# A two-layer conditioned trunk on one core: first shift vector summed with moving weight rows, and the convolution's shifted copies made by SBUF transfers

## The chip, the cores and the metric

The kernel runs on one core of a Trainium2 chip. The engines are TensorE (PE, with weight loads listed as PEld), VectorE (DVE), ScalarE (ACT), GpSimd (POOL) and SyncE (SP), which here only issues transfers. The metric is the device time in us of one execution, the median of the runs of a program. The kernel before took 1071.75 us (three runs, 1071.41 to 1072.74).

## The reference

Two layers over x of 256 positions by 1024 channels, float32. Each layer has three sub-layers on a modulated RMS norm: a SwiGLU feed-forward with half weight, a mixer, and a second feed-forward. The mixer of layer 0 is block attention with one block of 256 (its block selection is empty at this length), that of layer 1 is a Conformer convolution.

```python
c_act = jax.nn.silu(c)
mod = (c_act @ ada_w[i] + ada_b[i]).reshape(B, N_SUB, 3, D_MODEL)   # shift, scale, gate
pre(z, j) = rms_norm(z, norm_g[i, j]) * (1.0 + scl[:, j]) + shift[:, j]
x = x + 0.5 * gate[:, 0] * swiglu_ffn(pre(x, 0), ffn_w_in[i, 0], ffn_w_out[i, 0])
x = x + gate[:, 1] * mixer(pre(x, 1))
x = x + 0.5 * gate[:, 2] * swiglu_ffn(pre(x, 2), ffn_w_in[i, 1], ffn_w_out[i, 1])

def conformer_conv(h, ...):
    a, g = jnp.split(h @ w_pw1 + b_pw1, 2, axis=-1)
    u = a * jax.nn.sigmoid(g)
    u = depthwise_causal_conv(u, w_dw, width=31) + b_dw
    u = jax.nn.silu(layer_norm(u, ln_g, ln_b))
    return u @ w_pw2 + b_pw2
```

## The kernel before

All weights pass once through one ordered list, the stream, of tiles of 128 x 1024 float32 (512 KB) called `raw`, with six buffers. Python code sets the order by hand: `weave` mixes weight tiles with tiles of the modulation matrix `ada_w`, and each entry of the stream is issued on SP's queue as soon as the tile six places earlier is used up (`issue`, L188 to L204). `step` uses one entry: for a weight, ScalarE rounds it into a high part `whi` (L243) and VectorE subtracts to get the low part `wlo` (L218), so that `mm3` (L608 to L610) makes a float32 product of three rounded ones; for a modulation tile, VectorE folds its rows, weighted with silu(c), into `acc` (L279, L281). `need(unit)` steps until a unit is split, `block()` takes as many further steps as the current quota (`take(n)`) allows, and `run_sums` lets TensorE add up the 128 partitions of a finished `acc`. Split weights have a ring of six.

The start (`start`, `early_fold`, `early_sum`, `early_transposes`, `early_turn`) makes the first scale and shift vectors in four quarters of 256 columns. For each quarter four tiles arrive: scale rows in two tiles, shift rows in two, and then three weight tiles. VectorE folds both scale tiles and the first shift tile (twelve operations, L477 and L479). For the last shift tile TensorE takes each 128 x 128 piece as weights and one column of silu(c) as the moving side (L499). A matmul with a column of ones adds the partitions of `acc` (L500). In the first quarter `idle` puts matmuls on dummy data between these.

The convolution (`conv`) works on eight blocks of 128 channels. Blocks 0 to 3 are projected with positions on the partitions (`UT`) and turned (`across`), blocks 4 to 7 directly (`U`), into one of two PSUM banks `u`. `glu` applies sigmoid on ScalarE (L1009) and the product on VectorE (L1010) and writes `ub`, 128 channels by 288 positions with 30 zeros ahead. `spread` makes, for each group of 32 channels, four copies shifted by 0 to 3 positions on four partition groups of `R` (16 copies a block, eleven on VectorE, L1024, five on ScalarE, L1022). `wide` makes the filter tile `wd` on GpSimd (L963): taps on a diagonal mask. The depthwise block `C` is then 32 matmuls, each four taps times 32 channels against one channel group of `R` (L1033), and ScalarE adds the bias into `v`. `VT` transposes `v`; statistics, `norm`, `swish` and `put` prepare the input of the output projection `O`. Three buffers `ub`, two each of `R`, `wd` and `v`. The order of the loop over blocks:

```python
glu(b + 2); C(b); spread(b + 2); U(b + 4); wide(b + 2); VT(b - 1)
```

The second shift vector of layer 1's last feed-forward, `ada(4, (1, 2, 0))`, is woven between the convolution's weights.

## Time and profile before

| | |
|---|---|
| median of three runs | 1071.75 us |
| profiled execution, its own time | 1072.88 us |
| its span, first to last instruction | 1071.0 us |
| mean granted TensorE clock | 0.98 |
| busy: PE, PEld, DVE, ACT, POOL | 97%, 80%, 76%, 47%, 5% |
| HBM read | 248.24 MB, 233 GB/s over the span |

The busy shares are means over stages. The granted clock says how fast TensorE was allowed to run, as a share of 2.4 GHz; 0.5 is the lower level of 1.2 GHz. Durations of matmuls overlap, so the time that a group of them takes is read from where the group starts to where the next one starts.

### The profile page before, as it was taken

The numbers are of one execution on the slowest core, as the hardware profiler recorded it, in microseconds if no ns is written. First come the engines' busy times: TensorE is split into PE (matmuls) and PEld (weight loads), VectorE is DVE, ScalarE is ACT, GpSimd is POOL, SyncE is SP. The second block draws the span as 40 slices with busy tenths as digits, with TensorE's granted clock in tenths as the row PEclk, the third lists the DMA queues.
The fourth block names the chain that finished last, engine by engine and source line by source line (L and its number), as shares of the span: only waits on it lengthen the run. The fifth ranks groups of instructions, "written<-read, shape, count | busy, mean of one in ns | idle before, by whom it ended". The sixth has DMA issues, their size and how long they took to land.

```text
span 1071.0 us, 14807 instructions
## 1 busy us (share of the span) xinstructions
PE 1038.3 (97%) x5522; PEld 853.5 (80%) x5522; DVE 815.1 (76%) x1267; ACT 503.8 (47%) x794; POOL 53.2 (5%) x83
## 2 busy tenths in 40 slices
PE   8999999999999999999999999999988799999998
PEld 6888888877777788888878888888867588888886
DVE  5878878878997798778568788776789768665643
ACT  3354444555676544344354444454555446434430
POOL 3000000001210000000020000000211100000000
PEclk8999999999999999999999999999988899999999
DMA  8979998948767399898728889885545227776711
GB/s 297 297 244 340 307 324 296 332 160 260 248 205 221 101 324 313 281 311 293 251 88 311 284 296 317 284 289 159 164 149 195 86 65 238 270 230 199 236 40 39
DMA packets 181692, 250.26 MB, mean 234 GB/s; under 512 B 8389, under 2 KB 132070, under 8 KB 181620
## 3 DMA queue, kind: packets, MB, share of 16 engines
q1 hardware_dynamic: 180784, 248.55, 69.6%
q0 software_dynamic: 688, 0.71, 0.3%
q8 instruction: 43, 0.70, 0.2%
q14 instruction: 29, 0.24, 0.1%
q10 hardware_dynamic: 148, 0.06, 0.0%
HBM read 248.24 MB, written 1.05 MB: 233 GB/s over the span
## 4 chain that ended last, share of the span: by engine, by line
PE 87%; DVE 8%; issue 2%; ACT 1%; DMA 1%; POOL 1%; SPq 0%; DVEq 0%; POOLq 0%; ACTq 0%
PE u L608 15%; PE u L610 15%; PE u L609 14%; PE y L608 11%; PE y L610 11%; PE y L609 11%; DVE R L1024 2%; DVE wlo L218 2%; PE m L686 2%; PE m L322 1%; PE m L1033 1%; DMA raw<-in_ada_w_dram 1%; PE m L499 1%; DVE x L545 1%; PE m L587 1%
## 5 line engine op out<-in xcount | busy, mean ns | idle before, releaser
L218 DVE TENSOR_TENSOR wlo<-raw,whi 128x1024 fp32r<-128x1024 f32 x320 | 382.4, 1224 | 31.2 <-ACT whi L243 31.0
L243 ACT ACTIVATE whi<-raw 128x1024 fp32r<-128x1024 f32 x320 | 328.5, 1054 | 164.2 <-DMA raw<-in_ffn_w_in_dram 97.7
L608 PE MATMUL u<-whi,hh 128*128 128x512 f32 x672 | 266.5, 397 | 0.0
L610 PE MATMUL u<-whi,hl 128*128 128x512 f32 x672 | 262.7, 391 | 0.0
L609 PE MATMUL u<-wlo,hh 128*128 128x512 f32 x672 | 261.8, 390 | 0.0
L281 DVE SCALAR_TENSOR_TENSOR acc<-raw,sc,acc 128x512 f32<-128x512 f32 x224 | 169.5, 757 | 5.6 <-DMA raw<-in_ada_w_dram 0.7
L610 PEld LDWEIGHTS u<-whi,hl 128*128 128x128 f32 x672 | 126.1, 188 | 28.4 <-DVE hl L603 1.2
L608 PEld LDWEIGHTS u<-whi,hh 128*128 128x128 f32 x672 | 126.3, 188 | 25.5 <-ACT hh L602 0.6
L609 PEld LDWEIGHTS u<-wlo,hh 128*128 128x128 f32 x672 | 126.4, 188 | 25.1
L608 PE MATMUL y<-whi,gh 128*128 128x512 f32 x352 | 138.8, 394 | 0.2 <-ACT gh L694 0.2
L610 PE MATMUL y<-whi,gl 128*128 128x512 f32 x352 | 137.3, 390 | 0.0
L609 PE MATMUL y<-wlo,gh 128*128 128x512 f32 x352 | 137.1, 389 | 0.0
L695 DVE TENSOR_TENSOR gl<-m,gh 128x512 fp32r<-128x512 f32 (+1 forms) x48 | 31.1, 647 | 93.0 <-ACT gh L694 92.8
L608 PE MATMUL y<-whi,hh 128*128 128x512 f32 (+1 forms) x256 | 98.2, 384 | 0.0
L609 PE MATMUL y<-wlo,hh 128*128 128x512 f32 (+1 forms) x256 | 94.9, 371 | 0.0
L610 PE MATMUL y<-whi,hl 128*128 128x512 f32 (+1 forms) x256 | 94.7, 370 | 0.0
L694 ACT ACTIVATE gh<-m 128x512 fp32r<-128x512 f32 (+1 forms) x48 | 27.0, 562 | 132.4 <-PE m L686 132.4
L656 ACT ACTIVATE sg<-u 128x256 f32<-128x256 f32 x84 | 32.1, 382 | 113.9 <-PE u L610 113.9
L610 PEld LDWEIGHTS y<-whi,gl 128*128 128x128 f32 x352 | 66.1, 188 | 14.6 <-DVE gl L695 0.4
L608 PEld LDWEIGHTS y<-whi,gh 128*128 128x128 f32 x352 | 66.1, 188 | 13.8 <-ACT gh L694 0.7
L609 PEld LDWEIGHTS y<-wlo,gh 128*128 128x128 f32 x352 | 66.1, 188 | 13.3
L657 DVE TENSOR_TENSOR g<-u,sg 128x256 f32<-128x256 f32 x84 | 35.5, 422 | 35.0 <-ACT sg L656 34.6
(157 smaller groups left out, 984.4 us busy)
## 6 DMA issues: line engine op xcount, KB each, us to landing
raw<-in_ffn_w_in_dram SPq DMA_DIRECT2D x164, 512.0 KB, 5.0
raw<-in_ada_w_dram SPq DMA_DIRECT2D x144, 512.0 KB, 5.0
raw<-in_ffn_w_out_dram SPq DMA_DIRECT2D x88, 512.0 KB, 5.1
raw<-in_attn_w_qkv_dram SPq DMA_DIRECT2D x24, 512.0 KB, 4.8
raw<-in_conv_w_pw_dram SPq DMA_DIRECT2D x24, 512.0 KB, 4.9
raw<-in_ffn_w_in_dram SPq DMA_DIRECT2D x24, 256.0 KB, 5.5
raw<-in_attn_w_o_dram SPq DMA_DIRECT2D x8, 512.0 KB, 4.6
gate<-in_ada_b_dram SPq DMA_DIRECT2D x6, 512.0 KB, 6.7
```

The source lines that it names most:

```text
L218: (eng or nc.vector).tensor_tensor(lo, raw, hi.bitcast(F32), op=ALU.subtract)
L243: self.nc.scalar.activation(hi, self.like(self.raws[i], hi), AF.Copy)
L281: nc.vector.scalar_tensor_tensor(dst, raw[:, i, :], self.sc[:, k : k + 1], dst, op0=ALU.mult, op1=ALU.add)
L608: nc.tensor.matmul(out, lh, rh, start=start, stop=False)
L609: nc.tensor.matmul(out, lh, rl, start=False, stop=False)
L610: nc.tensor.matmul(out, ll, rh, start=False, stop=stop)
L656: nc.scalar.activation(sg, ps[:, 0:256], AF.Silu)
L657: nc.vector.tensor_tensor(gs[c][:, t, :], ps[:, 256:512], sg, op=ALU.mult)
L686: nc.tensor.transpose(ps[:, o : o + P], g[:, t, k * P : k * P + P], self.ident)
L694: nc.scalar.activation(hi, src, AF.Copy)
L695: nc.vector.tensor_tensor(lo, src, hi.bitcast(F32), op=ALU.subtract)
L1024: nc.vector.tensor_copy(dst, src)
```

## The change

In the start, only the two scale tiles are folded on VectorE. Both shift tiles stand as the moving side of TensorE: silu(c) is spread to 32 equal columns (`sc32`), which are the weights, and the 256 columns of a row block move through one of four column groups. The four partial rows (on partitions 0, 32, 64, 96) are copied to SBUF by ScalarE (`br`), and a matmul with the selecting column `pick` adds them and turns them onto partitions. The first quarter gets a second group of four idle matmuls. The two tiles of x are issued one weight tile earlier each.

In the convolution, `spread` issues 16 transfers from SBUF to SBUF, half on SP's queue, half on POOL's; `ub` and `R` get four buffers, `wd` and `v` three. All four gates of the first blocks come before the loop; the loop runs over four blocks and starts with the projection; the depthwise blocks 5, 6 and 7 are split into halves of 128 positions, each with a PSUM bank of its own. `b2` (the output bias) uses a buffer of the gates. The convolution's weights come first in the stream, and the eight tiles of the shift vector `(1, 2, 0)` last. The pad tile and the area for POOL's DMA descriptors get smaller.

```diff
--- before.py
+++ after.py
@@ -173,7 +173,9 @@
-        weave(pw1 + pw2, ada(4, (1, 2, 0)), 3)
+        for u in pw1 + pw2:
+            put(u)
+        stream.extend(ada(4, (1, 2, 0)))
...
         for i in range(RAW):
+            if i == 1:
+                nc.sync.dma_start(self.x[0], a["x"][0, 0:P, :])
-                nc.sync.dma_start(self.x[0], a["x"][0, 0:P, :])
-            if i == 3:
...
+        self.sc32 = self.fp.tile([P, KT, 64], F32, name="sc32")[:, :, 0:32]
+        nc.vector.tensor_copy(self.sc32, self.sc.unsqueeze(2).to_broadcast([P, KT, 32]))
+        self.pick = const.tile([P, 1], F32, name="pick")
+        nc.vector.tensor_reduce(
+            self.pick, self.ident.rearrange("p (k c) -> p k c", c=32)[:, :, 0], axis=AX.X, op=ALU.add
+        )
@@ -465,46 +472,61 @@
         nc = self.nc
-        accs = []
-        for e in range(3):
+        acc = self.fp.tile([P, 512], F32, name="acc", tag="acc", bufs=2)[:, 0:256]
+        shift = []
+        for e in range(4):
             raw = self.raws[self.taken].rearrange("p (k n) -> p k n", k=4)
-            if e != 1:
-                acc = self.fp.tile([P, 512], F32, name="acc", tag="acc", bufs=2)[:, 0:256]
-                accs.append(acc)
+            self.taken += 1
+            self.high = max(self.high, self.taken)
+            if e >= 2:
+                shift.append(raw)
+                continue
             for i in range(4):
-                k = 4 * (e % 2) + i
+                k = 4 * e + i
                 if k == 0:
                     nc.vector.tensor_scalar(acc, raw[:, i, :], self.sc[:, k : k + 1], None, op0=ALU.mult)
                 else:
                     nc.vector.scalar_tensor_tensor(
                         acc, raw[:, i, :], self.sc[:, k : k + 1], acc, op0=ALU.mult, op1=ALU.add
                     )
             self.issue()
+        return acc, shift
...
+        def scale(ps):
+            for i in range(2):
+                nc.tensor.matmul(ps[:, i : i + 1], acc[:, i * P : i * P + P], self.one, start=True, stop=True)
+
+        rows = self.bank("m" if q else "y")
+        if not q:
+            ps = self.bank("m")
+            scale(ps)
+        for e, raw in enumerate(shift):
+            if not q:
                 idle(IDLE_SUMS)
...
+            for k in range(4):
+                nc.tensor.matmul(
+                    rows[32 * k : 32 * k + 32, 0:256], self.sc32[:, 4 * e + k, :], raw[:, k, :],
+                    start=e == 0, stop=e == 1,
+                )
+            self.issue()
+        br = self.two.tile([P, 256], F32, name="br", tag="sq", bufs=1)
+        nc.scalar.activation(br, rows[:, 0:256], AF.Copy)
+        pt = self.early_transposes(q)
+        if q:
+            ps = self.bank("m")
+            scale(ps)
+        for i in range(2):
+            nc.tensor.matmul(ps[:, 2 + i : 3 + i], br[:, i * P : i * P + P], self.pick, start=True, stop=True)
...
-        ub = [cp.tile([P, 288], F32, name=f"ub{i}") for i in range(3)]
+        ub = [cp.tile([P, 288], F32, name=f"ub{i}") for i in range(4)]
-        us, R, wd, cs, yv, st, mv, rs = {}, {}, {}, {}, {}, {}, {}, {}
+        us, R, wd, yv, st, mv, rs = {}, {}, {}, {}, {}, {}, {}
-            wd[b] = cp.tile([P, 8, 4, 32], F32, name="wd", tag="wd", bufs=2)
+            wd[b] = cp.tile([P, 8, 4, 32], F32, name="wd", tag="wd", bufs=3)
@@ -1013,21 +1035,17 @@
         def spread(b):
-            u = ub[b % 3]
-            R[b] = cp.tile([P, 4, 284], F32, name="R", tag="R", bufs=2)
+            u = ub[b % 4]
+            R[b] = cp.tile([P, 4, 284], F32, name="R", tag="R", bufs=4)
             for g in range(4):
                 for j in range(4):
-                    dst, src = R[b][32 * j : 32 * j + 32, g, :], u[32 * g : 32 * g + 32, j : j + 284]
-                    if 4 * g + j in (1, 4, 7, 10, 13):
-                        nc.scalar.activation(dst, src, AF.Copy)
-                    else:
-                        nc.vector.tensor_copy(dst, src)
+                    eng = nc.sync if (g + j) % 2 else nc.gpsimd
+                    eng.dma_start(R[b][32 * j : 32 * j + 32, g, :], u[32 * g : 32 * g + 32, j : j + 284])
         def C(b, t0=0, n=T):
-            if b not in cs:
-                cs[b] = self.bank("m")
-                us["v", b] = cp.tile([P, T], F32, name="v", tag="v", bufs=2)
-            ps = cs[b][:, t0 : t0 + n]
+            if ("v", b) not in us:
+                us["v", b] = cp.tile([P, T], F32, name="v", tag="v", bufs=3)
+            ps = self.bank("m")[:, 0:n]
             for q in range(8):
                 for g in range(4):
                     nc.tensor.matmul(
...
-        b2 = cp.tile([P, D], F32, name="b2")
+        b2 = self.two.tile([P, D], F32, name="b2", tag="gate")
...
-        wide(0), wide(1)
@@ -1115,44 +1132,40 @@
         UT(w[1][:, 256:], 2, 1)
         across(0, 1, e, 0), across(1, 1, e, 256)
         e = evac(w[1])
-        glu(0), spread(0)
+        glu(0), spread(0), wide(0)
         UT(w[3][:, 256:], 3, 1)
         f = evac(w[3])
         across(2, 0, e, 0), across(2, 1, e, 256)
-        glu(1), spread(1)
+        glu(1), spread(1), wide(1)
+        across(3, 0, f, 0), across(3, 1, f, 256)
+        glu(2), spread(2), wide(2)
+        glu(3), spread(3)
         take(PUMP_LOOP)
-        for b in range(6):
-            if b >= 4:
-                self.block()
-            if b:
-                glu(b + 2)
+        for b in range(4):
+            U(b + 4)
+            glu(b + 4)
             C(b)
-            if not b:
-                across(3, 0, f, 0), across(3, 1, f, 256)
-                glu(b + 2)
-            spread(b + 2)
-            if b + 4 < 8:
-                U(b + 4)
-            wide(b + 2)
+            spread(b + 4), wide(b + 3)
             if b:
                 VT(b - 1)
-            if b == 1:
-                nc.vector.tensor_tensor(b2, b2, gate, op=ALU.mult)
-            elif b in (2, 3):
-                x = self.x[b - 2]
-                nc.vector.tensor_tensor(x, x, b2, op=ALU.add)
+                if b == 1:
+                    nc.vector.tensor_tensor(b2, b2, gate, op=ALU.mult)
+                else:
+                    x = self.x[b - 2]
+                    nc.vector.tensor_tensor(x, x, b2, op=ALU.add)
         nc.scalar.activation(warm, self.mhalf, AF.Silu)
-        self.need(self.pw2[2])
+        self.block()
+        C(4), wide(7), VT(3)
+        self.need(self.pw2[3])
+        take(5)
+        C(5, 0, P), VT(4), self.block(), C(6, 0, P), VT(5, (0,)), C(7, 0, P), VT(6, (0,))
+        C(5, P, P), VT(7, (0,)), moments(0), norm(0, 0), norm(0, 1)
         take(0)
-        C(6, 0, P), VT(5), C(7, 0, P), C(6, P, P), VT(6, (0,)), VT(7, (0,))
-        moments(0), norm(0, 0), norm(0, 1)
-        C(7, P, P), VT(6, (1,)), swish(0, 0), VT(7, (1,)), moments(1), put(0, 0)
+        C(6, P, P), VT(5, (1,)), C(7, P, P), VT(6, (1,)), swish(0, 0), VT(7, (1,)), moments(1), put(0, 0)
+        self.run_sums(True)
         swish(0, 1), norm(1, 0), put(0, 1), norm(1, 1)
         O(0, 0), swish(1, 0), O(0, 1), put(1, 0), swish(1, 1), put(1, 1), take()
-        O(0, 2)
-        self.need(self.pw2[3])
-        self.run_sums(True)
-        O(0, 3)
+        O(0, 2), O(0, 3)
         self.residual(0, y[0], gate, 1.0)
         O(1, 0), O(1, 1)
         after()
...
-    nc = _bacc.Bacc("TRN2", target_bir_lowering=False, num_devices=1)
+    nc = _bacc.Bacc("TRN2", target_bir_lowering=False, num_devices=1, dynamic_dma_scratch_size=8192)
```

Three places show what moves. On POOL, between the set-up of the convolution's buffers and its statistics, before (`ub` is the gated input, `b` the output bias, `wd` the filter):

```order
L956 MEMSET ub_6567 128x30
L957 MEMSET ub_6567 128x2
L1100 DMA b_6575<-in_conv_b_pw_dram 128x1024
L963 TENSOR_TENSOR wd<-w_4927,mask 128x1024 x8
L1059 TENSOR_TENSOR lr_7683<-lr_7683,mhalf 128x1
```

The same place now:

```order
L1118 DMA b_6578<-in_conv_b_pw_dram 128x1024
L1043 DMA R<-ub_6565 32x284 x8
L985 TENSOR_TENSOR wd<-w_4927,mask 128x1024
L1043 DMA R<-ub_6566 32x284 x8
L985 TENSOR_TENSOR wd<-w_4927,mask 128x1024
L1043 DMA R<-ub_6567 32x284 x8
L985 TENSOR_TENSOR wd<-w_4927,mask 128x1024
L1043 DMA R<-ub_6568 32x284 x8
L1043 DMA R<-ub_6565 32x284 x8
L985 TENSOR_TENSOR wd<-w_4927,mask 128x1024
L1043 DMA R<-ub_6566 32x284 x8
L985 TENSOR_TENSOR wd<-w_4927,mask 128x1024
```

Each filter now stands behind the eight transfers of a block; the filters of blocks 3 to 6 stand behind the transfers of the block after them.

On VectorE, from the gate of block 0 to that of block 3, before (`wlo` is the low part of a split weight, `acc` a fold):

```order
L1010 SCALAR_TENSOR_TENSOR ub_6565<-u,cols,sg 128x256
L1024 COPY R<-ub_6565 32x284 x11
L218 TENSOR_TENSOR wlo<-raw,whi 128x8x128 x2
L1010 SCALAR_TENSOR_TENSOR ub_6566<-u,cols,sg 128x256
L1024 COPY R<-ub_6566 32x284 x11
L1010 SCALAR_TENSOR_TENSOR ub_6567<-u,cols,sg 128x256
L1024 COPY R<-ub_6567 32x284 x11
L281 SCALAR_TENSOR_TENSOR acc<-raw,sc,acc 128x512 x2
L218 TENSOR_TENSOR wlo<-raw,whi 128x8x128 x2
L279 TENSOR_SCALAR acc<-raw,sc 128x512
L281 SCALAR_TENSOR_TENSOR acc<-raw,sc,acc 128x512
L218 TENSOR_TENSOR wlo<-raw,whi 128x8x128
```

The same place now:

```order
L1032 SCALAR_TENSOR_TENSOR ub_6565<-u,cols,sg 128x256
L220 TENSOR_TENSOR wlo<-raw,whi 128x8x128 x2
L1032 SCALAR_TENSOR_TENSOR ub_6566<-u,cols,sg 128x256
L1032 SCALAR_TENSOR_TENSOR ub_6567<-u,cols,sg 128x256
L1032 SCALAR_TENSOR_TENSOR ub_6568<-u,cols,sg 128x256
L220 TENSOR_TENSOR wlo<-raw,whi 128x8x128
L220 TENSOR_TENSOR wlo<-raw,whi 128x1024 x4
L1032 SCALAR_TENSOR_TENSOR ub_6565<-u,cols,sg 128x256
```

The four gates follow each other with two splits between them, and no copy is left.

On TensorE, the sums of the second quarter of the first modulation, before (`z` is the normed x, `y` a hidden block's PSUM bank):

```order
L500 MATMUL m<-one,acc 128x1 x2
L499 MATMUL m<-sc,raw 128x1 x4
L500 MATMUL m<-one,acc 128x1
L499 MATMUL m<-sc,raw 128x1 x4
L500 MATMUL m<-one,acc 128x1
L516 MATMUL m<-ident,z 128x128 x4
L608 MATMUL y<-whi,hh 128x512
```

The same place now:

```order
L511 MATMUL m<-raw,sc_158 32x256 x8
L538 MATMUL m<-ident,z 128x128 x4
L501 MATMUL m<-one,acc 128x1 x2
L523 MATMUL m<-pick,br 128x1 x2
L630 MATMUL y<-whi,hh 128x512
```

Eight matmuls with 256 moving columns replace eight with one column and two sums; the selecting matmuls stand behind the transposes and the scale's sums.

## Rows read from the trace of the kernel before

**Rows 1.** the page's first part: busy us of each engine, with its share of the span, and its number of instructions.

```profile
PE 1038.3 (97%) x5522; PEld 853.5 (80%) x5522; DVE 815.1 (76%) x1267; ACT 503.8 (47%) x794; POOL 53.2 (5%) x83
```

**Rows 2.** whom TensorE waited for, over the whole span: engine, line and output tile of the waiting instruction, then engine, tile and line of the one it waited for; us in total, times, longest.

```profile
PE u L608 <- DVE ub L1010: 9.2, 2, 5.0
PE m L1033 <- DVE R L1024: 4.3, 5, 2.6
```

**Rows 3.** windows of the convolution stage: from and to in us of the span, length, busy us (and instructions) of TensorE's matmuls, its weight loads, VectorE, ScalarE and GpSimd, then the granted TensorE clock as a share of full speed, the mean busy share of the DMA engines, and GB/s. 792.05 to 798.22 and 806.91 to 815.75 each hold one projection block and two transposes, 815.75 to 819.34 one depthwise block, and 851.06 to 855.18 what lies between the last depthwise matmul and the first output matmul.

```profile
792.05:798.22 6.17, 6.17 (x54) 6.00 (x51) 5.87 (x12) 5.94 (x10) 1.97 (x1) 1.00 0.41 158
...
806.91:815.75 8.84, 8.84 (x51) 8.67 (x51) 8.59 (x17) 6.43 (x10) 0.00 (x0) 0.65 0.46 147
...
815.75:819.34 3.59, 3.59 (x66) 1.98 (x65) 2.29 (x3) 0.00 (x0) 0.00 (x0) 1.00 0.88 266
...
837.23:851.06 13.83, 12.49 (x261) 9.52 (x261) 8.42 (x25) 5.34 (x12) 0.56 (x1) 0.76 0.04 17
...
851.06:855.18 4.12, 2.59 (x22) 2.00 (x19) 3.75 (x9) 2.84 (x9) 0.55 (x1) 1.00 0.02 4
...
769.72:855.18 85.46, 70.15 (x881) 55.35 (x879) 74.53 (x136) 43.84 (x82) 12.85 (x8) 0.88 0.43 143
```

**Rows 4.** TensorE in order of time, from 771 to 781: start, length, engine, line, operation, output and input tile, shapes, how many; in brackets the idle time before it and what ended it.

```profile
771.68 3.61 PE L1033 MATMUL m<-R,wd 128*32 128x256 f32 x58 [0.37 <-DVE R L1024]
...
775.22 0.66 PE L1001 MATMUL u<-ident,z 128*128 128x128 f32 x4
...
780.04 0.58 PE L608 MATMUL u<-hh,whi 128*128 128x256 f32 x1 [4.16 <-DVE ub L1010]
```

**Rows 5.** VectorE in order of time in the same stretch (columns as in the group before).

```profile
767.44 0.48 DVE L1010 SCALAR_TENSOR_TENSOR ub<-u,cols,sg 128x256 f32<-128x256 f32 x1 [2.68 <-ACT sg L1009]
...
773.84 0.48 DVE L1010 SCALAR_TENSOR_TENSOR ub<-u,cols,sg 128x256 f32<-128x256 f32 x1
...
774.42 5.05 DVE L1024 COPY R<-ub 32x284 f32<-32x284 f32 x11
```

**Rows 6.** groups of instructions by line between 740 and 900 us: line, engine, operation, tiles, shapes, count, then busy us and mean ns of one, then the idle time before them and what ended it.

```profile
L1024 DVE COPY R<-ub 32x284 f32<-32x284 f32 x88 | 32.6, 370 | 5.4 <-PE m L1033 3.5
...
L1022 ACT ACTIVATE R<-ub 32x284 f32<-32x284 f32 x40 | 17.5, 438 | 18.2 <-DVE ub L1010 17.6
...
L963 POOL TENSOR_TENSOR wd<-w,mask 128x1024 f32<-128x1024 f32 x8 | 15.6, 1955 | 67.7 <-PE m L1033 67.7
...
L993 ACT ACTIVATE z<-y 128x512 f32<-128x512 f32 x4 | 2.4, 592 | 4.5 <-PE y L610 4.5
...
L1009 ACT ACTIVATE sg<-u,cols 128x256 f32<-128x256 f32 x8 | 3.7, 462 | 0.0
...
L1010 DVE SCALAR_TENSOR_TENSOR ub<-u,cols,sg 128x256 f32<-128x256 f32 x8 | 3.8, 480 | 2.7 <-ACT sg L1009 2.7
```

**Rows 7.** GpSimd (POOL) in order of time: the last of nine small transfers at the start, the first four of the loads of the convolution taps, and one filter `wd`.

```profile
10.28 0.49 POOL L385 DMA_DIRECT2D rows<-in_attn_g_k_dram  x1 [1.72 <-DMA ab<-in_ada_b_dram]
...
556.87 2.27 POOL L931 DMA_DIRECT2D tq<-in_conv_w_dw_dram  x4 [0.29 <-POOL tq L927]
...
775.44 1.99 POOL L963 TENSOR_TENSOR wd<-w,mask 128x1024 f32<-128x1024 f32 x1 [18.58 <-PE m L1033]
```

**Rows 8.** DMA issues by line: tiles, issuing queue, count, KB each, median us from issue to landing. The first row is of the window 755 to 860, the second of the whole span.

```profile
raw<-in_conv_w_pw_dram SPq DMA_DIRECT2D x13, 512.0 KB, 4.6
...
tq<-in_conv_w_dw_dram POOLq DMA_DIRECT2D x7, 16.0 KB, 3.4
```

**Rows 9.** the instructions that touch the raw weight tiles in the window 755 to 860: count, then shortest, median and longest in ns, first and last start, shapes.

```profile
L218 DVE TENSOR_TENSOR wlo<-raw,whi x20: 1212/1220/2865, 761.0 to 833.1; 128x1024 fp32r<-128x1024 f32 x20
...
L281 DVE SCALAR_TENSOR_TENSOR acc<-raw,sc,acc x14: 744/752/2397, 758.7 to 813.5; 128x512 f32<-128x512 f32 x14
...
L203 SPq DMA_DIRECT2D raw<-in_conv_w_pw_dram x13: 327/340/368, 759.5 to 811.7; - x13
```

**Rows 10.** the same view for VectorE's copies into the tile `R`.

```profile
L1024 DVE COPY R<-ub x88: 295/300/1926, 768.0 to 844.8; 32x284 f32<-32x284 f32 x88
```

**Rows 11.** groups by line in the window 20 to 60 us (columns as in group 6).

```profile
L479 DVE SCALAR_TENSOR_TENSOR acc<-raw,sc,acc 128x256 f32<-128x256 f32 x30 | 14.5, 485 | 1.1
...
L243 ACT ACTIVATE whi<-raw 128x1024 fp32r<-128x1024 f32 x10 | 10.5, 1052 | 18.4 <-DMA raw<-in_ffn_w_in_dram 18.4
...
L528 ACT ACTIVATE hf<-m,mod,mod 128x256 f32<-128x256 f32 x6 | 3.1, 562 | 4.8 <-PE m L516 4.8
```

**Rows 12.** TensorE in order of time at the sums of the second quarter of the first modulation: the matmuls on the last shift tile for 128 columns, and the sum of VectorE's part.

```profile
28.01 1.03 PE L499 MATMUL m<-sc,raw 128*128 128x1 f32 x8
...
28.90 0.36 PE L500 MATMUL m<-one,acc 128*128 128x1 f32 x2
```

**Rows 13.** windows of the start (columns as in group 3). 30.63 to 35.05, 43.48 to 46.33 and 55.22 to 59.65 hold the twelve matmuls of the third hidden block, one window for each quarter, right behind the sums of the next.

```profile
30.63:35.05 4.42, 4.42 (x15) 3.51 (x14) 3.48 (x6) 2.60 (x4) 0.00 (x0) 0.61 0.90 285
...
35.05:40.49 5.44, 5.44 (x25) 4.50 (x24) 5.08 (x13) 0.65 (x1) 0.00 (x0) 1.00 1.00 336
...
43.48:46.33 2.85, 2.85 (x16) 2.34 (x15) 2.04 (x4) 2.51 (x4) 0.00 (x0) 1.00 0.83 257
...
55.22:59.65 4.43, 4.43 (x16) 3.50 (x14) 2.03 (x4) 2.60 (x4) 0.00 (x0) 0.61 0.90 308
```
## What was predicted

> **What bounds the kernel now.** The page's busy shares come first: TensorE is busy for 97% of the span [rows 1], so an edit pays only where TensorE stands still, runs at its low clock, or loses an instruction of its own. The list of who TensorE waited for comes next [rows 2]: two waits for the gated convolution input `ub` make 9.2 us and five for its shifted copies `R` make 4.3 us, all in one stage. So the third view is a table of windows over that stage [rows 3]. From 769.72 to 855.18 it takes 85.46 us, TensorE is busy for 70.15 of them, and the granted clock is 0.88. The longest wait for `ub` is 5.0 us [rows 2], and the projection behind it, 806.91 to 815.75, takes 8.84 us at clock 0.65, where the one in 792.05 to 798.22 takes 6.17 us at 1.00 [rows 3]. A pause is so paid twice: itself, and some 2.5 us at the lower of the two clock levels (1.2 GHz) behind it. Last come the two engines' order of time around the other pause, of 4.16 us [rows 4], and what VectorE does in front of it [rows 5]: `ub` of block 1 ends at 774.3, eleven copies run until 779.47, and only then comes `ub` of block 2, which frees the PSUM bank that the projection of block 4 needs. The page's line groups give the size: 88 copies of 370 ns on VectorE (32.6 us), 40 of 438 ns on ScalarE (17.5 us) [rows 6].
>
> **The convolution, step by step.** The floor is TensorE's own work at full clock. Four projections with a pair of transposes each: 4 x 6.17 = 24.7 us. Eight depthwise blocks: 8 x 3.59 = 28.7 us. Four more transpose pairs of some 0.3 us (6.17 less the 5.9 of a bare projection, an estimate): 1.2. Two groups of transposes into the banks: some 1.0, at 0.66 for four [rows 4]. The tail from the last depthwise matmul to the first output matmul: 4.12 us. One column sum that ran inside a projection before and now stands in the tail: 1.0. Durations without a group are in [rows 3]. Sum 60.7 us, so at most 85.5 - 60.7 = 24.8 us can go.
>
> What is late next? All 128 copies leave both engines and become 128 transfers, 64 on SP's queue and 64 on POOL's, four buffers deep.
>
> POOL first, since it also makes the filters `wd` between them. A POOL transfer costs 0.49 to 0.57 us of issue: four took 2.27 us in one row, a single one 0.49 [rows 7]. A filter takes 1.96 us [rows 6]. A block is 8 x 0.55 + 1.96 = 6.4 us, eight blocks 51 us. Starting when `ub` of block 0 is written (767.9) [rows 5], POOL ends at 819. TensorE consumes a block in 6.17 + 3.59 = 9.8 us, so POOL is ahead in the loop and is met again only at its end, where three depthwise blocks follow without a projection: I allow 1 us there. Each transfer waits for the one eight places earlier to land; landing takes 3.4 us for small ones from POOL [rows 8], less than the 6.4 us of a turn.
>
> SP next: eight transfers a block at about the 0.34 us of a weight issue [rows 9] are 2.7 us, with at most five weight issues behind them (1.7 us), 4.4 of the 9.8 us available. The transfers of block b+4 wait on SP for the depthwise block b, and what is queued behind them is the weights of the next block, six raw tiles ahead of need; nobody waits for those at once. A transfer issued behind weights lands like them, 4.6 us after issue [rows 8]; it is needed three blocks, some 29 us, later. That cover is absent for block 0 alone: its last POOL issue is at 772.3, landing 775.7, filter ready 774.3, while the projection of block 4, in front of its depthwise block, ends near 778. [...]
>
> Then the banks. Projections have two PSUM banks; the gate of block 2 waits for transposes that wait for block 1's. ScalarE's copy (0.6), sigmoid (0.46) and VectorE's product (0.48) [rows 6] make about 1.2 us of pause ahead of the first projection, instead of 4.16.
>
> VectorE keeps 5 steps per block. A split costs 1.22 us, a fold of a late vector's tile 2 x 0.75 [rows 9]: at most 5 x 1.5 = 7.5, with the product 0.48 and up to 2 us held up by a filter some 10 us in the last blocks, against 9.8. The product has a bank in hand, so I take zero; the bound is 2 us. The late vector's steps all stand before the last projection ends, so its sums are ready in the tail.
>
> Each depthwise block now starts behind 16 transfer semaphores, four on each of four matmuls. No row shows such a start; bounds are 0 and the 0.37 us that TensorE lost where it waited for the copies within a block [rows 4], eight times that being 3.0 us. I take 1.5, halfway, since no row is nearer. Losses: 1.0 + 1.2 + 1.5 = 3.7. Gain 24.8 - 3.7 = 21.1 us.
>
> A row speaks on the POOL half in another way. A copy on VectorE takes 0.295 us at least and 1.926 at most [rows 10], and the long ones begin where a filter begins on POOL (775.44) [rows 7]: the two engines held each other up. The Trainium skill, page "SBUF — State Buffer", section "SBUF: two separate sides", says that a VectorE copy in a fast mode and a GpSimd operation exclude each other for the whole instruction, and gives about 3.1 us for a POOL-issued DMA beside such a copy, where one alone takes 0.62. By that, an estimate from the page, 64 issues would cost 198 us. The trace agrees on the filter, and on the tap loads it shows 2.27 us for four issues beside VectorE's splits, with no such stretch [rows 7]; and the change removes the copies. So the sum goes by 0.55.
>
> **The start.** Per quarter of the first modulation, VectorE loses four folds of 0.485 us [rows 11], 1.9 us. TensorE loses eight one-column matmuls and two sums (the trace shows each as two passes), two runs of 1.03 + 0.36 [rows 12]; it gains eight matmuls with 256 columns in groups of 32 (a quarter of the 3.59 us of a depthwise block's 32: 0.9 us) and two sums (0.4). Per quarter 2.8 - 1.3 = 1.5 us less. Against it stands ScalarE's copy `br`, queued ahead of two weight splits of 1.05 us; by the sigmoid of the same size it takes 0.46, so the modulation (two of 0.56 us) [rows 11] starts some 2.5 us after the sums instead of at once. TensorE, with one 2.85 us block as cover [rows 13], stalls about 0.5 us. Two of three quarters also show the low clock behind the one-column matmuls: 4.42 and 4.43 us at 0.61, against 2.85 at 1.00 [rows 13]. I count on getting back half of one, 0.8 us. Weight arrival limits it: the DMA engines are 0.83 to 1.00 busy in these windows [rows 13]. The first quarter is a draw: `x` comes one tile sooner, the second scale tile later, and four more idle matmuls stand on TensorE. Sum: 3 x 1.0 + 0.8 = 3.8 at best in TensorE's terms; with arrival I take 2. Bounds: +2 (first quarter delayed, no clock gained) and -5 (three quarters at 1.5, no drop). The smaller pad and descriptor area and the bias's new place cost nothing: they free space, and the bias is still fetched ahead of the first projection and used in the loop.
>
> Total: 21 + 2 = 23 us. The profiled execution took 1072.88 us for a span of 1071.0; 1072.88 - 23 = 1049.9. The median of the runs is 1.1 us lower, so 1049.
>
> **Rivals.** (1) The transfers become the wait in some blocks. For: weights and copies share the DMA engines, 0.43 busy in the stage before [rows 3], with 4.7 MB more (128 x 32 x 284 x 4 bytes) in less time. Against: four buffers. Two late blocks with 3 us of pause and 2.5 us of low clock each, and 2 us at the start: gain 21 - 11 = 10, time 1062.
>
> (2) POOL sets the pace and the kernel is slower. Behind the last filter stand half blocks of 1.8 us (4 x 1.8), transposes and the tail, 12 us; equal time is reached if the last filter is ready at 843, so (843 - 768 - 8 x 1.96) / 64 = 0.93 us per issue decides. For: the one issue that waited for the transfer eight places earlier stood 1.72 us [rows 7], and this wait now comes 56 times. Against: it stood behind a saturated queue, and 1.72 per turn of eight gives 8.1 us a block, still under 9.8. At 1.2 us an issue: 8 x (9.6 + 1.96) = 92, end at 872, 17 us later: 1089. The skill's rule is the extreme of this case.
>
> (3) The stage shrinks but the time doesn't, since the weights set the pace of what follows. For: DMA was idle from 837 on and TensorE ran on prefetched weights [rows 3]. Against: full buffers then, which are full again. Time 1071.
>
> **Chances.** The forecast 0.66 (its own range 1042 to 1055: 24.8 + 5 off the median at best, 21 - 6 with no gain at the start at worst), rival 1 0.20, rival 2 0.10, rival 3 0.04. The range of 1042 to 1064 takes in rival 1 and leaves out rivals 2 and 3 and a little of the edges. A change under 0.2%, some 2 us, can't be told from none. Faster 0.86, same 0.04, slower 0.10.
>
> **What would show it.** In the profile after: no copies `R` on VectorE or ScalarE; the two waits for `ub` near 1 us; granted clock 0.97 or more and four projections near 6 us; POOL's transfers near 0.55 us with filters between; from the first projection to the first output matmul some 62 us. At the start: eight matmuls of about 0.9 us per quarter, and windows behind them at clock 1.00. A depthwise block that waits for a DMA by microseconds speaks for rival 1, POOL issues over 0.93 us for rival 2, output matmuls that wait for weights for rival 3.

## The result and the profile after

| | median, us | range, us |
|---|---|---|
| kernel before (same chip) | 1071.58 | 1071.10 to 1072.74 |
| changed kernel | 1064.20 | 1063.25 to 1065.08 |

The ratio is 0.9929, with a 95% interval of 0.9912 to 0.9947. The kernel is 7.4 us faster, where 23 were forecast. The profiled execution took 1063.98 us, for a span of 1062.2. Of the runs of the experiments below one, of `half_count`, took 2627.02 us in a slow state and is left out of that kernel's ratio.

The page's busy shares, against [rows 1]:

```profile
span 1062.2 us, 15077 instructions
...
PE 1029.1 (97%) x5590; PEld 839.5 (79%) x5590; DVE 786.7 (74%) x1165; ACT 487.3 (46%) x759; POOL 87.6 (8%) x149
```

Who TensorE waited for, against [rows 2] (us in total, times, longest):

```profile
PE y L1065 <- ACT v L1055: 12.1, 2, 9.1
PE m L708 <- DVE g L679: 4.1, 3, 1.4
...
PE u L630 <- ACT hh L553: 1.2, 3, 0.4
PE u L1023 <- DVE ub L1032: 1.1, 1, 1.1
```

The two waits that the prediction attacked are gone but for the one of 1.1 us that it left. A new one heads the list: a transpose of the depthwise result `v`, twice, 12.1 us. Windows of the convolution stage, cut as in the last row of [rows 3] and up to the first output matmul, and of the end of that stage (columns as there):

```profile
764.96:845.16 80.20, 65.28 (x946) 52.43 (x943) 53.19 (x57) 22.54 (x37) 49.80 (x72) 0.89 0.67 211
...
812.00:831.00 19.00, 9.52 (x133) 7.77 (x133) 14.88 (x14) 7.15 (x11) 8.90 (x10) 0.56 0.73 228
```

The stage takes 80.20 us instead of 85.46. The loss sits at its end, where TensorE is busy for half of 19 us at clock 0.56. Cutting the stage at the end of the depthwise block of channel block 4, the last full one, shows it best. TensorE there, before:

```profile
830.56 3.66 PE L1033 MATMUL m<-R,wd 128*32 128x256 f32 x64 [0.24 <-ACT v L1037]
...
849.17 1.96 PE L1033 MATMUL m<-R,wd 128*32 128x128 f32 x64
...
855.18 0.48 PE L608 MATMUL y<-whi,hh 128*128 128x512 f32 x1
```

and after:

```profile
805.76 3.66 PE L1051 MATMUL m<-R,wd 128*32 128x256 f32 x64
...
818.54 0.69 PE L1065 MATMUL y<-ident,v 128*128 128x128 f32 x2 [9.12 <-ACT v L1055]
819.16 4.06 PE L1051 MATMUL m<-R,wd 128*32 128x128 f32 x64
826.16 0.69 PE L1065 MATMUL y<-ident,v 128*128 128x128 f32 x2 [2.94 <-ACT v L1055]
826.77 4.05 PE L1051 MATMUL m<-R,wd 128*32 128x128 f32 x64
```

Before, block 4 ends 64.5 us into the stage (769.72 to 834.22), after, 44.5 us (764.96 to 809.42): the loop gained 20.0 us. From there to the first output matmul (855.18; 845.16) it took 21.0 us and now takes 35.7: 14.8 us given back. Of these 12.1 are the two waits; the half depthwise blocks behind them take 4.06 and 4.05 us instead of the 1.96 of the last half block before (849.17), at the low clock (0.56 in the second window).

What held `v`? ScalarE at this place:

```profile
816.70 1.06 ACT L245 ACTIVATE whi<-raw 128x1024 fp32r<-128x1024 f32 x1 [20.39 <-DMA raw<-in_ffn_w_in_dram]
817.67 0.46 ACT L1031 ACTIVATE sg<-u,cols 128x256 f32<-128x256 f32 x1
818.02 0.47 ACT L1055 ACTIVATE v<-m,cols 128x256 f32<-128x256 f32 x1
```

The program order has a look-ahead step, the split of the next feed-forward's first weight tile, ahead of the last gate's sigmoid and of `v`. ScalarE stood 20.39 us in it, waiting for the tile. And why was the tile late? SyncE's transfers:

```profile
763.24 5.06 SPq L1043 DMA_DIRECT2D R<-ub  x8
768.41 0.98 SPq L205 DMA_DIRECT2D raw<-in_conv_w_pw_dram  x2
769.49 16.18 SPq L1043 DMA_DIRECT2D R<-ub  x24
785.78 1.50 SPq L205 DMA_DIRECT2D raw<-in_conv_w_pw_dram  x3
787.37 0.99 SPq L205 DMA_DIRECT2D raw<-in_ada_w_dram  x2
788.72 8.61 SPq L1043 DMA_DIRECT2D R<-ub  x8
...
806.58 0.49 SPq L205 DMA_DIRECT2D raw<-in_ffn_w_in_dram  x1
807.44 9.77 SPq L1043 DMA_DIRECT2D R<-ub  x8
```

The copies of blocks 1 to 3 keep SyncE for 16.18 us in one piece, with conv weights behind them; each later eight takes 5 to 10 us, their waits included. The tile is issued at 806.58, and ScalarE has it 10.1 us later. That second part is long as well: in `four_dma`, below, it is 5.8 us (796.20 to 802.05). Here four modulation tiles go out in the 2 us just ahead of it (804.43 to 806.49); whether they hold it up wasn't tested. The issues of one line (min/median/max ns):

```profile
L1043 SPq DMA_DIRECT2D R<-ub x64: 507/588/1298, 763.2 to 829.7; - x64
L1043 POOL DMA_DIRECT2D R<-ub x64: 496/496/529, 763.8 to 822.6; - x64
```

GpSimd's are 0.50 us, close to the forecast of 0.55; SyncE's are 0.59, not 0.34. The start, TensorE in the first quarter, with a window behind the sums of each later quarter, against [rows 13]:

```profile
16.84 2.99 PE L404 MATMUL y<-ones 128*128 128x512 f32 x12
19.84 0.50 PE L630 MATMUL u<-whi,hh 128*128 128x512 f32 x1
```

```profile
28.26:31.27 3.01, 3.01 (x14) 2.16 (x13) 2.66 (x5) 2.32 (x4) 0.00 (x0) 1.00 0.89 288
40.12:43.13 3.01, 3.01 (x14) 2.15 (x13) 2.66 (x5) 2.24 (x4) 0.00 (x0) 1.00 1.01 350
51.92:54.93 3.01, 3.01 (x14) 2.15 (x13) 2.66 (x5) 2.38 (x4) 0.00 (x0) 1.00 0.96 332
```

The first projection starts at 19.84 us (before: 22.18), and the block behind each later quarter's sums runs at clock 1.00, where two of three had 0.61 [rows 13].

### The profile page after: what moved, and what is told of

Same layout as the page of the kernel before. It is cut to its first block, busy times and chain, and to the rows that moved or that the text cites. A ratio compares the mean times of both kernels' runs of the same rounds, so it can differ in the third digit from the quotient of the medians.

```text
span 1062.2 us, 15077 instructions
## 1 busy us (share of the span) xinstructions
PE 1029.1 (97%) x5590; PEld 839.5 (79%) x5590; DVE 786.7 (74%) x1165; ACT 487.3 (46%) x759; POOL 87.6 (8%) x149
## 5 line engine op out<-in xcount | busy, mean ns | idle before, releaser
L220 DVE TENSOR_TENSOR wlo<-raw,whi 128x1024 fp32r<-128x1024 f32 x320 | 390.3, 1249 | 49.4 <-ACT whi L245 49.4
L678 ACT ACTIVATE sg<-u 128x256 f32<-128x256 f32 x84 | 32.1, 382 | 114.3 <-PE u L632 114.3
L632 PEld LDWEIGHTS y<-whi,gl 128*128 128x128 f32 x352 | 66.1, 188 | 14.6 <-DVE gl L717 0.4
L586 POOL TENSOR_TENSOR r<-v,mhalf 128x1 f32<-128x1 f32 x12 | 6.6, 554 | 680.6 <-DVE v L585 680.5
```

Source lines behind the costliest of these rows:

```text
L220: (eng or nc.vector).tensor_tensor(lo, raw, hi.bitcast(F32), op=ALU.subtract)
L586: nc.gpsimd.tensor_tensor(r, v, self.mhalf[:, 0:1], op=ALU.pow)
L632: nc.tensor.matmul(out, ll, rh, start=False, stop=stop)
L678: nc.scalar.activation(sg, ps[:, 0:256], AF.Silu)
```

## The experiments

All ratios are against the kernel before on the same chip. The theories: QUEUE (SyncE's issues of the copies hold up the weights), SHARING (copies and weights share the DMA engines), SPLIT (the look-ahead step on ScalarE is itself the cost), POOL (GpSimd's issues).

**The two parts alone.** `start_only` is the kernel before with the new start; `conv_only` the changed kernel with the old one.

> The kernel before with the start of the change alone (shift tiles as the moving side, x one tile earlier, the smaller pad and descriptor area); the convolution is that of before. If the start gives what the trace of the changed kernel shows at 64 us (the ninth hidden block's end there 4.0 us earlier) and nothing later takes it back, the time is 1067 to 1068. My term of the prediction was 2 us (1069.7). If what is won at the start is lost again because weights set the pace, 1071.

> The changed kernel with the start of before. If the two parts add up, the convolution's part is worth the rest, 7.4 - 4.5 = 3 us: 1068 to 1069, with the same 9 us wait of TensorE for `v` behind the depthwise block 4. If the long wait depends on how early the start ended (it should not), the time differs.

1066.68 us, ratio 0.9962 (0.9948 to 0.9976), and 1070.89, 0.9998 (0.9988 to 1.0007). The start gives 4 us; the convolution alone gives nothing. Alone the two give some 3 us less than the 7.4 together, a little more than the intervals leave room for. In `conv_only` the wait for `v` is 14.6 us (12.1 in the change), and from the end of block 4 to the output matmuls it takes 38.7 us (35.7); why an earlier start makes this shorter stays open.

**SPLIT.** `no_look` leaves out the look-ahead from the last projection on, and the steps between the half blocks (the lines that set the look-ahead to 0 are not printed here):

```
-        take(5)
-        C(5, 0, P), VT(4), self.block(), C(6, 0, P), ...
+        C(5, 0, P), VT(4), C(6, 0, P), ...
```

> The changed kernel without looking ahead for a split from the projection of block 7 on, and without the two further blocks of steps behind the loop: no split of the feed-forward's weights stands on ScalarE ahead of the gate of block 7 and of `v` of blocks 3 to 7. Theory SPLIT (that order on ScalarE is the cause by itself): the waits of 9.1 and 2.9 us and the low clock behind them go, some 15 us, 1049 to 1051. Theory QUEUE (SP issues a copy transfer in 0.59 us where I counted 0.34, the weights stand behind 24 of them from 769.5 to 785.7, the whole stream runs late, and so do the copies of blocks 6 and 7, which stand behind late weights on SP and wait for their landing): the depthwise blocks 6 and 7 still wait for their copies, and VectorE's gate of block 7 for the late modulation tiles, so only 3 to 6 us go, 1058 to 1061.

1066.27 us, 0.9962 (0.9951 to 0.9974): slower than the change, and outside the forecasts of both theories. SPLIT falls: the wait only moved. TensorE now waits for a filter:

```profile
PE m L1051 <- POOL wd L985: 10.9, 2, 9.9
```

GpSimd makes that filter behind the transfers of block 7, which wait for its gate, which stands on VectorE behind folds of modulation tiles that were just as late.

**Order.** `weights_first` issues the copies of blocks 2 and 3 behind the loop's first projection, so that the conv weights go ahead of them:

```
-        glu(2), spread(2), wide(2)
-        glu(3), spread(3)
+        glu(2)
+        glu(3)
...
+            if not b:
+                spread(2), wide(2), spread(3)
```

> The changed kernel with the copies of blocks 2 and 3 issued behind the weights that the first projection of the loop takes, so that five weight tiles pass SP ahead of sixteen copy transfers. Theory QUEUE: the stream runs some 8 us earlier through the stage, the first tile of the next feed-forward lands near 808 instead of 816.7, the 9.1 us wait shrinks to 0 to 2 and the time falls by 8 to 14 us, 1050 to 1056. Theory SHARING (weights land late because the copies share the DMA engines, not because of the order on SP): less than 2 us change, 1062 to 1066. Theory SPLIT alone gives the same fall as QUEUE only if the tile's lateness comes from SP.

1063.48 us, 0.9935 (0.9911 to 0.9958): no gain over the change. Five conv weights do go ahead (773.4 to 777.5), but the run of 24 copies follows and the first feed-forward tile is issued at 806.70, as late as ever. QUEUE's forecast failed, and the time is the one that SHARING gave; the next run decides between the two. Moving the run of copies behind five weights only moved it ahead of the tiles that came next.

**Count.** `half_count` moves the same bytes in eight transfers a block (two groups from one source, so half of the channels are copies of the wrong rows).

```
-            for g in range(4):
+            for g in range(0, 4, 2):
...
+                    eng = nc.sync if j % 2 else nc.gpsimd
+                    src = u[32 * g : 32 * g + 32, j : j + 284].unsqueeze(1).to_broadcast([32, 2, 284])
+                    eng.dma_start(R[b][32 * j : 32 * j + 32, g : g + 2, :], src)
```

> The changed kernel with eight copy transfers a block instead of sixteen, four on each queue, of twice the size: each writes one channel group's shifted rows into two places of the copy tile, so half of the convolution's channels are computed from wrong rows; bytes and instructions other than the issues stay. Theory QUEUE (SP is full: 64 issues of about 0.6 us and the weights' issues and landings between them from 763 to 831): SP's copy issues take 20 us less, the tile of the next feed-forward is issued some 10 us earlier, the waits of 9.1 and 2.9 us and their low clock go: 1047 to 1052. Theory SHARING (bytes on the DMA engines): no change beyond 2 us, 1062 to 1066.

1052.59 us, 0.9811 (0.9783 to 0.9839), with three of the four runs between 1047.63 and 1052.74. Same bytes, half of the issues on each queue, some 12 us: the number of issues, not SHARING. Which of the two queues it is, this run doesn't tell.

**Other engines for SyncE's half.** `pool_11` gives GpSimd 11 and SyncE 5 of 16; `hybrid` does SyncE's eight as copies, five on VectorE and three on ScalarE; `act_queue` issues them from ScalarE.

```
pool_11:   eng = nc.sync if 4 * g + j in (1, 4, 7, 10, 13) else nc.gpsimd
act_queue: eng = nc.scalar if (g + j) % 2 else nc.gpsimd
```

> The changed kernel with five of a block's sixteen copies on SP's queue and eleven on POOL's (eight and eight before). POOL then issues 88 transfers of 0.5 us and eight filters of 2 to 3 us, some 64 us of the stage, SP 40 instead of 64. Theory QUEUE: weights come earlier by up to 24 x 0.6 = 14 us, the long wait goes; POOL at 5.5 + 2.4 = 7.9 us a block stays under TensorE's 9.8: 1050 to 1056. Theory POOL (rival 2 of the prediction, the queue of POOL is near its limit, since its filters already take 2.9 us beside VectorE): depthwise blocks wait for filters, 1062 to 1070.

> The changed kernel with no copies on SP's queue: eight of a block's sixteen by POOL's transfers as before, five by VectorE's copies (0.30 us each) and three by ScalarE's (0.44 us each). Theory QUEUE: weights are issued as in the kernel before, the split of the next feed-forward finds its tile, no wait of more than 2 us in the stage: 1046 to 1052. If VectorE's copies and POOL's issues hold each other up by more than a copy's length (the rule on the shared port, with 3.1 us an issue as its page has it), POOL ends its filters late and the time is 1065 or more.

> The changed kernel with SP's half of the copies issued from ScalarE's queue instead, nothing on SP. Theory QUEUE: weights are on time as in hybrid, but ScalarE pays 64 issues; at SP's 0.6 us they are 4.8 us a block beside some 6 us of splits, gates and biases, 10.8 against TensorE's 9.8, so part of the gain goes to late gates: 1052 to 1060. If an issue from ScalarE holds it for under 0.2 us, 1046 to 1052.

1064.48 us (ratio 0.9940, 0.9923 to 0.9957), 1062.09 (0.9917, 0.9900 to 0.9934) and 1079.35 (1.0085, 1.0061 to 1.0108). With 11 the wait for `v` is gone, and GpSimd is the limit instead:

```profile
PE m L1051 <- POOL wd L985: 13.3, 4, 4.3
```

That is rival 2, reached with 11 issues a block, not with 8. ScalarE as issuer holds its own gates: TensorE waits 11.5 us for `ub` and 19.3 for `v`.

`hybrid` has no copy on SyncE's queue and still misses QUEUE's forecast by 10 us. SyncE there:

```profile
786.71 18.43 SPq L205 DMA_DIRECT2D raw<-in_ada_w_dram  x8
806.34 23.65 SPq L205 DMA_DIRECT2D raw<-in_ffn_w_in_dram  x8
```

The tile goes out as late as in the change (806.58), for another reason. VectorE's copies stand between the first gates, so `ub` of block 3 is begun at 776.63 instead of 767.74, ScalarE's next splits start at 778.59 instead of 767.60, and raw buffers come free later. Block 4 ends at 816.42 instead of 809.42, and then TensorE waits 7.6 us for `v`, which stands on ScalarE behind its own three copies of block 7; these begin at 820.14, when VectorE has written `ub`. So a full SyncE queue is not the only way to make the stream late.

**Four transfers a block.** `four_dma` lets one transfer carry a group's 32 rows to all four shifts: the source is read four times, each time one element on, and the copy's rows lie four shifts to a channel. Taps and mask are laid out likewise.

```
-                for j in range(4):
-                    eng = nc.sync if (g + j) % 2 else nc.gpsimd
-                    eng.dma_start(R[b][32 * j : 32 * j + 32, g, :], u[32 * g : 32 * g + 32, j : j + 284])
+                eng = nc.sync if g % 2 else nc.gpsimd
+                src = u[32 * g : 32 * g + 32, 0:284].unsqueeze(1).to_broadcast([32, 4, 284])
+                src = type(src)(src.tensor, src.offset, [src.ap[0], (1, 4), (1, 284)])
+                eng.dma_start(R[b][:, g, :], src)
```

> The changed kernel with four transfers a block instead of sixteen: one transfer carries a group's 32 rows to all four shifts at once (128 rows of the copy, the source read four times, each time one element further on), two from SyncE and two from GpSimd. The rows of the copy then lie four shifts to a channel, so the filter's weights, their mask and the taps are laid out in the same order (one strided copy of the taps on GpSimd). Same bytes, same result, a quarter of the issues. QUEUE (SyncE's issues of half a microsecond each are the cost, whatever they carry): SyncE's transfers of the stage fall from 64 of 0.59 to 16, some 38 us to 9, the first tile of the next feed-forward is issued by 795, the waits of 9.1 and 2.9 us on ScalarE are gone and their low clock too: 1047 to 1054, the conv stage under 69 us. BYTES (the copies' traffic or the number of rows that a transfer cuts out sets the time): SyncE's transfers take about four times as long each, 2 us, and the time stays at 1060 to 1066.

1045.54 us, 0.977 (0.9750 to 0.9791): 25 us faster than before and better than both kernels. A transfer of 128 rows takes hardly longer to issue than one of 32 (median 596 against 588 ns on SyncE, 548 against 496 on GpSimd):

```profile
L1048 SPq DMA_DIRECT2D R<-ub x16: 554/596/1486, 763.4 to 807.9; - x16
L1048 POOL DMA_DIRECT2D R<-ub x16: 546/548/589, 763.9 to 808.2; - x16
```

The first feed-forward tile is issued at 796.20, and block 4 is followed by half blocks without a pause:

```profile
805.89 3.66 PE L1056 MATMUL m<-R,wd 128*32 128x256 f32 x64
...
809.86 1.95 PE L1056 MATMUL m<-R,wd 128*32 128x128 f32 x64
...
827.76 0.47 PE L630 MATMUL y<-whi,hh 128*128 128x512 f32 x1
```

The loop ends where it did in the change (809.55 against 809.42); from there to the output matmuls it is 18.2 us instead of 35.7. ScalarE still stands 5.61 us for that tile, but has it at 802.05, before the result of block 3 that it turns into `v` is ready.

**Which issues?** `late_copies` takes SyncE's half of blocks 4 to 7 back to VectorE and ScalarE. `sp_few` has two large transfers on SyncE and eight small ones on GpSimd, `pool_few` the reverse.

```
late_copies: elif b < 4: nc.sync.dma_start(dst, src)   (else ScalarE or VectorE copies)
sp_few:      if g % 2 == 0: for j in range(4): eng.dma_start(R[b][j:128:4, g, :], u[...])
pool_few:    if g % 2:      the same
```

> The changed kernel, where blocks 4 to 7 take SyncE's eight transfers of a block as copies on VectorE (five) and ScalarE (three); blocks 0 to 3 and GpSimd's half are as in the change. QUEUE: SyncE loses 32 issues, about 19 us, between 788 and 831, the next feed-forward's first tile is issued near 793 instead of 806.6, and v of block 3 and the gate of block 7 no longer stand behind its split: 1049 to 1056. The copies cost VectorE 1.5 and ScalarE 0.9 us a block of 9.6, which have room in the loop, though they stand between the gates of blocks 4 to 7 and may bring back 1 us of waits. SHARED ENGINES (the copies put back what the change took from VectorE and ScalarE, and cost as much as the queue): 1060 to 1066.

> The version with four transfers a block, but GpSimd's half again as eight transfers of 32 rows; SyncE keeps two of 128 rows. SYNC (the time was lost to SyncE's issues, behind which the weights stood): as good as with four, 1045 to 1050. POOL (it was GpSimd's issues, behind which the filter matrices stood): back to 1058 to 1066. BOTH: 1051 to 1057.

> The reverse: SyncE's half again as eight transfers of 32 rows a block, GpSimd's two of 128 rows. SYNC: back to 1058 to 1066, with the waits on ScalarE for the next feed-forward's first tile (some 9 us) and the half clock behind them. POOL: 1045 to 1050. BOTH: 1051 to 1057.

1058.88 us (0.9891, 0.9874 to 0.9907), 1054.40 (0.9844, 0.9827 to 0.9860) and 1062.96 (0.9916, 0.9892 to 0.9939). The trace of `late_copies` corrects QUEUE as I had put it. SyncE:

```profile
768.06 17.49 SPq L1046 DMA_DIRECT2D R<-ub  x24
785.66 1.47 SPq L205 DMA_DIRECT2D raw<-in_conv_w_pw_dram  x3
787.22 16.02 SPq L205 DMA_DIRECT2D raw<-in_ada_w_dram  x8
804.44 23.69 SPq L205 DMA_DIRECT2D raw<-in_ffn_w_in_dram  x8
```

Not one copy stands there after 785.66, and the tile still goes out at 804.44: the issues now wait for raw buffers, since the splits and folds that free them run late. So the first 32 issues are enough to make the stream late. That those of blocks 4 to 7 add little isn't shown, since the copies that replace them take time of VectorE and ScalarE, which do the splits and folds. They bring a wait of their own, too: of the 12.5 us that TensorE waits for `v` here, only the first 3.50 come behind the tile.

```profile
811.43 0.44 PE L1072 MATMUL y<-ident,v 128*128 128x128 f32 x2 [3.50 <-ACT v L1062]
...
824.42 0.69 PE L1072 MATMUL y<-ident,v 128*128 128x128 f32 x2 [8.95 <-ACT v L1062]
```

```profile
818.32 1.33 ACT L1048 ACTIVATE R<-ub 32x284 f32<-32x284 f32 x3 [6.94 <-issue]
```

In the other 8.95 us `v` stands behind ScalarE's copies of block 7, as in `hybrid`. The trace names no releaser for these; VectorE's `ub` of that block ends at 818.24, just before.

Both queues count. By the ratios, SyncE relieved alone gives 9 of the 17 us between the change and `four_dma`, and then GpSimd's filter is waited for. GpSimd relieved alone gives about 1, within the noise (its profiled execution took 1058.62 us, the other three 1062.74 to 1063.77):

```profile
PE m L1060 <- POOL wd L989: 4.4, 1, 4.4
...
PE y L1074 <- ACT v L1064: 2.5, 1, 2.5
```

```profile
PE y L1074 <- ACT v L1064: 10.4, 2, 6.8
```

(`sp_few`, then `pool_few`.) One number goes with the wait for `v` in these runs: how long before the end of block 4 the first feed-forward tile is issued.

| run | tile ahead of block 4's end, us | wait for `v`, us | block 4's end to output, us |
|---|---|---|---|
| before | 21.4 | 0.2 | 21.0 |
| four_dma | 13.4 | 0 | 18.2 |
| sp_few | 12.9 | 2.5 | 26.8 |
| half_count | 11.0 | 2.5 | 22.4 |
| hybrid | 10.1 | 7.6 | 27.2 |
| pool_few | 4.0 | 10.4 | 32.1 |
| late_copies | 3.5 | 12.5 | 33.5 |
| changed kernel | 2.8 | 12.1 | 35.7 |
| conv_only | 1.4 | 14.6 | 38.7 |
| weights_first | 1.1 | 11.8 | 35.3 |
| no_look | 1.0 | 0 | 34.4 |

It doesn't order them strictly. `sp_few` waits 4.4 us for a filter as well, `no_look` 10.9 us for filters in place of `v`, and in `hybrid` and `late_copies` most of the wait for `v` is behind ScalarE's copies. In `pool_11`, `act_queue` and `weave_back` block 4 itself begins 7 to 13 us late, so they are left out here. QUEUE's forecasts of times were too low in `no_look`, `weights_first`, `pool_11`, `hybrid`, `act_queue` and `late_copies`: relief of SyncE brought up the next thing that stood ahead of its data. What carries QUEUE are the runs that change the number of issues and not the engine: `half_count`, `four_dma`, `sp_few` and `pool_few`.

**The late vector.** `weave_back` puts its eight tiles between the conv weights again.

```
-        for u in pw1 + pw2:
-            put(u)
-        stream.extend(ada(4, (1, 2, 0)))
+        weave(pw1 + pw2, ada(4, (1, 2, 0)), 3)
```

> The changed kernel with the one modulation vector's eight tiles woven between the convolution's weights again, as before the change, instead of behind them. As predicted (the place of the vector costs nothing, because nobody waits for its steps): within 2 us of the change, 1062 to 1066. QUEUE with the full SyncE after 763: whatever of the eight tiles is issued ahead of the transfers leaves about 4 us of SyncE between 787 and 806, so the next feed-forward's first tile comes up to 4 us sooner and the wait of 9.1 us shrinks by as much, but the convolution's own weights come later by eight tiles of about 1.3 us: the waits on ScalarE move to blocks 4 to 7. Net 1058 to 1070.

1062.90 us, 0.9928 (0.9913 to 0.9943), as with the change. The wait for `v` falls to 4.5 us, and TensorE stands 7.1 us more in front of block 4's depthwise matmuls, where the trace names no releaser. What holds them there stays open; the place of the vector seems to say only which work comes late.

**The start's filling matmuls.** `no_fill` and `four_nofill` take out the eight filling matmuls between the first quarter's sums, of the change and of `four_dma`.

```
-            if not q:
-                idle(IDLE_SUMS)
```

> The changed kernel without the eight filling matmuls ahead of the two moved-row sums of the first quarter (the twelve behind them stay). One look for the start alone, read from the trace. CLOCK (the first quarter gained 2.3 us because TensorE stays busy from 10.4 to 19.8 and has the full clock for the twelve matmuls and for the first projection): without the eight, TensorE idles between the sums, the clock stays at the lower level from 12 to 20, and the first projection starts at 21 to 22 instead of 19.84. ARRIVAL (it gained because the scale tiles come in another order and the sums are shorter): the start stays within 0.5 us of 19.84.

> The version with four transfers a block, without the eight filling matmuls of the first quarter. In the look at the change without them the first projection started at 17.69 instead of 19.84 with the full clock all the way, so neither of the two theories on the clock and on the arrival held as stated. If the 2.15 us at the start stay to the end: 1043 to 1044. If the later quarters only wait for their tiles that much longer (ARRIVAL sets the pace of the start): 1045 to 1046, and the transposes that follow the last quarter begin within 0.5 us of where they did.

`no_fill`: 1062.19 us in one execution, first projection at 17.69, and the twelve last filling matmuls at full speed (2.99 us). `four_nofill`: 1045.72, 0.9756 (0.9738 to 0.9775), the same as `four_dma` (1045.54); there those twelve took 4.92 us, and the first projection starts at 19.70, where `four_dma` has 18.04. CLOCK falls as a reason for the first quarter's gain: it forecast a start at 21 to 22 us without the fillers, and even at the low clock the start is some 2.4 us ahead of the old one. Nor do the fillers bring anything that can be measured in the time of the kernel. ARRIVAL, as a start within 0.5 us of 19.84, holds in the one and not in the other. Across the profiles of 13 kernels with the new start and its fillers the first projection starts at 18.0 to 20.1 us, in the two with the old start at 22.05 and 22.18. Why it comes earlier than forecast stays open.

## Why the prediction was half right

- **The loop: right.** Projections of 6.0 us, depthwise blocks of 3.66, one pause of 1.1 (forecast 1.2), gained 20.0 us up to block 4. The price of 1.5 us for sixteen semaphores a block was too high: the blocks took 3.66 us, as an undisturbed one did before (830.56), so no cost shows.
- **GpSimd's 0.55 us an issue: right** at 0.50. The allowance of 1 us at the end was never tested in the change, because another wait came first; `sp_few` shows it at 4.4 us.
- **SyncE, "eight transfers a block at about the 0.34 us of a weight issue": wrong, and the step that failed.** A copy between two places in SBUF took 0.59 us to issue, and up to 1.3. I priced it from the nearest instruction by name, a weight load. By the sum of the prediction this would still have been 4.7 + 1.7 = 6.4 of 9.8 us a block. So the size of the issue alone doesn't break the forecast; the stretch that was summed does. The copies of blocks 0 to 3 stand ahead of the loop, 32 in a row but for two weights, with no 9.8 us a block to hide in: SyncE is taken up by them from 763.24 to 785.67.
- **"Nobody waits for those at once": wrong, the other half of that step.** Block 4 ends 24.8 us sooner than before (809.42, before 834.22; 20.0 of it in the loop, the rest ahead of it), so the first tile behind it was needed that much sooner, and it was issued only 6.2 us sooner (806.58, before 812.82). ScalarE takes its program in order, so the split that stood 20.39 us for its tile kept back the last gate and `v`. The prediction counted the lead in tiles ("six raw tiles ahead of need") and never asked when the next stage's first tile would be issued.
- **Rival 1 came nearest**, at 1062, but by another way: the trace of the change names no wait of a depthwise block for a copy. Rival 3, that weights set the pace of what follows, had the mechanism, with a time for no gain at all; the loss is 14.8 us, not all. Its sign, output matmuls that wait for weights, didn't show: the wait came earlier, at `v`.
- **The start: undersized.** 2 us forecast, 4 measured alone. The `br` stalls were right (1.2 us over three quarters against some 1.5), and so was the clock, but it came back in both quarters where I took half of one. The first quarter, "a draw", gained 2.3 us.
- The range of the forecast was added up wrongly at its upper end: 21 - 6 = 15 us off 1071.75 is 1057, not 1055.
- With a quarter of the issues and the same loop, `four_dma` takes 1045.5, 3.5 us below the forecast of 1049; the start, 4 us alone against 2 forecast, accounts for some 2 of these.

## What to carry to other kernels

When a loop gets shorter, find the first thing of the next stage that an in-order engine will wait for, and work out when its transfer is issued now and when it is needed then. Price each DMA by the issues on its queue, ahead of the loop as well as in it, and let one access pattern carry many small copies before moving them to another engine. If two queues are both near the limit, relieving one alone can show half of the gain (SyncE here) or almost none (GpSimd). And work put back on an in-order engine can itself stand ahead of what is needed, as ScalarE's copies did in `hybrid` and `late_copies`.

## What the hardware showed that I had not expected

- An issue costs by the transfer and hardly by its rows: 0.59 us on SyncE for 32 rows and 0.60 for 128, 0.50 and 0.55 on GpSimd. SyncE's were the slower.
- GpSimd's issues were not stretched by VectorE's copies: in `hybrid` eight of them took 4.14 us from 775.74 on, while VectorE made five copies from 777.22 to 782.02, and the longest of all 64 took 0.66 us. It was the copies that grew: three of the five took 0.30 us, two 1.92 and 1.93, the first of them from 778.2 on, before the filter's record begins at 779.90; why stays open. The rule weighed in the prediction (the Trainium skill, "SBUF — State Buffer", section "SBUF: two separate sides") gives some 3.1 us for an issue beside a VectorE copy whose length it doesn't state; no issue here comes near that. The section also says that a VectorE operation with two SBUF inputs and a GpSimd operation that reads SBUF exclude each other. With that the trace agrees: in the changed kernel the filter takes 2.3 us on average, with VectorE's splits beside it, and 1.9 us alone.
